# A transformer block with a state-space mixer, sparse attention and a mixture of experts: expert weights of four by row blocks and column quarters, the first w_in blocks in float32, powers by doubling

## The chip, the cores and the metric

The kernel runs on one core of a Trainium2 chip. A core has five engines with queues of their own: TensorE (PE, matrix products into PSUM; its weight loads are listed apart as PEld), VectorE (DVE), ScalarE (ACT), GpSimd (POOL) and SyncE (SP), which here issues nearly all DMA transfers. Each engine takes its instructions in order, and a semaphore holds an instruction back until what it reads is there. The metric is the device time of one execution in microseconds (us); smaller is better. All data are float32 in HBM.

## The reference

One layer over 256 tokens of width 1024, in four steps, cut to what matters:

```
mod = silu(c) @ ada_w + ada_b                 # six vectors of 1024: sh1, sc1, g1, sh2, sc2, g2
h = rms_norm(x) * (1 + sc1) + sh1
proj = h @ w_in                               # q, six kv parts, gates, u (state space), merge gates
x = x + g1 * (g_attn * (attn @ w_o) + g_ssm * (ssm @ ssm_w_o)) @ w_out
h = rms_norm(x) * (1 + sc2) + sh2
x = x + g2 * moe(h)                           # 32 experts in 4 groups, the top group, 2 experts of it
return rms_norm(x)
```

`ssm` is a diagonal complex recurrence over the tokens (32 groups, 64 states each), written by the kernel as short convolutions and a scan over powers of the diagonal. `attn` is compressed, selected and windowed attention. Each expert computes `(silu(x @ w_gate) * (x @ w_up)) @ w_down` with an inner width of 256. All 32 experts together have 96 MB of weights (3 MB each), and all of them are read in every execution.

## The kernel before

The program is one function, `hybrid`, and a planner of the framework turns it into one list per engine: it runs the program on simulated times and puts ready instructions in the order in which they come up there. So the order on an engine isn't the order of the lines, and an edit in one place can move instructions in others. Buffers are tiles of pools; a tile that takes the memory of an older one waits until all readers of the older one are done. `room` (L69) hands out loads of 1 MB in turn from a list of such slots (`set_rings`), and `load` (L92) issues the transfer on SP's queue.

*The front.* The loop at L128 issues eight modulation blocks (`ada1_k`, 1 MB: two vectors for one 128-wide slice of the model) and eight row blocks of the first four column groups of w_in (`slab`, 128x1024 each, two to a slot): u0, u1 (input of the state-space part), kc and vc (compressed keys and values). They share the five slots of `ringA`. The loop at L375 takes the row blocks k = 0 to 7 in turn. `mod_sum` (L236) multiplies the modulation block with silu(c), eight products in four column groups of TensorE at once, and `mod_end` (L245) turns the sums upright and makes the scale Gm and the shift modT. Then the normed input, turned earlier into xnT, becomes hf = xnT * Gm + modT (L378). Products of the projections are done in three passes of a faster 4-byte type, float32r: `mm3` (L286) adds high x high, high x low and low x high, for which hf is split into hTh and hTl (L379, L380) and the row block into a pair of `whi` and `wlo` halves (L382 on ScalarE, L383 on VectorE). Per row block these are eight triples of 256 columns. Later projections split their weights in the same way in `split` (L272 to L284).

Beside it the constants of the state-space part are made: VectorE and POOL build the discretised matrices (L418 to L531), `cmul` (L472 to L478) makes complex powers in a chain, six instructions each: `pows` to the fourth power (three products), `pk4` to the eighth power of that (seven) and two squarings `sq`. Vc gets 20 copies of 64x256 (L574 to L580), four on ScalarE and sixteen on VectorE. The front ends with the products of L563, which need U (the projections of u0 and u1) and Wt.

*The middle.* Keys, compression (`blk`, L710 to L719: four windows of keys and values, with a column of zeros that POOL sets), the scan, attention by four chunks (L862 on), and output projections, up to `wout`. A matrix `perm` (L976) orders the tokens; it is read at L1057.

*The experts.* Nine blocks (BLOCKS): seven quads of experts with 32 places each and two pairs with 64, in the order quad, quad, pair, quad, pair, four quads. The ring has 21 slots of 1 MB. For each expert a quad loads gate and up weights in two halves of four row blocks each (`egu`, [128, 4, 512]), all first halves and then all second ones, and the down weights in one tile (`edn`, [128, 2, 1024]): twelve loads. For the last quad the second halves come as two pieces of 512 KB per expert, and the down weights as two column halves. `ffn_block` (L1183) does, for each row block k, one product per expert (four side by side in TensorE's columns, L1192), the activation (L1200 to L1202), the down product in two halves of 512 columns (L1215), the weighting (L1218), and adds the result to the four accumulators `acc` (L1224). After the last block come the squares (L1317), the last norm and four output transfers (L1359).

```
for e, h in order_[:n_e] if last else order_:
    egu[e][h] = load(A["egu"][e0 + e][:, 4 * h:4 * h + 4], [4, 512], f"gu{e0 + e}{h}")
```

## Time and profile before

| | |
|---|---|
| median of three runs | 599.57 us (598.16 to 601.19) |
| the profiled execution | 600.95 us, span 599.1 us |
| TensorE busy | 526.7 us (88%) |
| VectorE busy | 343.1 us (57%) |
| ScalarE, POOL busy | 200.2 and 201.4 us (33 and 34%) |
| moved by DMA | 168.11 MB, mean 281 GB/s |
| mean granted TensorE clock | 0.963 |

The span runs from the first to the last instruction; the execution's own time is 1.85 us longer. A busy share is a mean over stages with different limits, so each stage is read by itself. In rows of instruction groups the columns are line, engine, operation, written tile and read tiles, shapes and count, then busy time and mean duration in ns, then the idle time just before them and what ended it. A float32 matmul is two records in the trace, one of float32r is one.

### The profile page before, as it was taken

The numbers are of one execution on the slowest core, as the hardware profiler recorded it, in microseconds if no ns is written. First come the engines' busy times: TensorE is split into PE (matmuls) and PEld (weight loads), VectorE is DVE, ScalarE is ACT, GpSimd is POOL, SyncE is SP. The second block draws the span as 40 slices with busy tenths as digits, with TensorE's granted clock in tenths as the row PEclk, the third lists the DMA queues.
The fourth block names the chain that finished last, engine by engine and source line by source line (L and its number), as shares of the span: only waits on it lengthen the run. The fifth ranks groups of instructions, "written<-read, shape, count | busy, mean of one in ns | idle before, by whom it ended". The sixth has DMA issues, their size and how long they took to land.

```text
span 599.1 us, 10825 instructions
## 1 busy us (share of the span) xinstructions
PE 526.7 (88%) x4173; PEld 369.1 (62%) x4174; DVE 343.1 (57%) x942; ACT 200.2 (33%) x461; POOL 201.4 (34%) x299
## 2 busy tenths in 40 slices
...
GB/s 328 318 259 143 220 132 123 354 209 275 157 198 185 133 107 75 266 171 127 112 363 392 244 323 370 264 339 422 418 418 421 421 421 420 420 419 421 413 344 74
DMA packets 28443, 168.11 MB, mean 281 GB/s; under 512 B 3171, under 2 KB 3299, under 8 KB 11363
## 3 DMA queue, kind: packets, MB, share of 16 engines
...
q14 instruction: 22, 0.17, 0.1%
...
## 4 chain that ended last, share of the span: by engine, by line
PE 52%; DVE 19%; issue 10%; DMA 8%; POOL 7%; ACT 3%; SPq 0%; POOLq 0%; ACTq 0%; DVEq 0%
PE guq L1192 9%; PE pgq L1163 5%; PE dnq L1215 5%; DMA adt<-in_adat_dram 4%; PE acc L1224 4%; DMA fg<-in_fg_dram 3%; POOL adt L354 2%; DVE wlo L282 2%; DVE wlo L383 2%; PE p L291 2%; PE p L290 2%; PE y L799 2%; PE p L289 2%; POOL pr L919 2%; DMA slab<-in_w_dram 1%
## 5 line engine op out<-in xcount | busy, mean ns | idle before, releaser
L1356 POOL TENSOR_TENSOR x<-x,fg 128x512 f32<-128x512 f32 x1 | 1.3, 1267 | 263.6 <-ACT x L1355 263.6
L1192 PE MATMUL guq<-gu,room__4521 128*32 128x512 f32 (+1 forms) x480 | 69.5, 611 | 3.2 <-DMA gu<-in_egu_dram 2.2
L1167 DVE TENSOR_SCALAR room__4521<-pgq,Gm,modT 128x128 f32<-128x128 f32 x36 | 14.7, 409 | 71.5 <-PE pgq L1163 36.2
L1163 PEld LDWEIGHTS pgq<-room__4521,x 128*128 128x128 f32 x288 | 37.9, 197 | 23.2 <-issue 10.1
L1165 ACT ACTIVATE room__4521<-pgq,modT,Gm 128x128 f32<-128x128 f32 x36 | 16.5, 460 | 98.7 <-PE pgq L1163 90.8
L1163 PE MATMUL pgq<-room__4521,x 128*128 128x128 f32 x288 | 45.0, 296 | 4.0 <-DVE room__4521 L1167 1.9
L1192 PEld LDWEIGHTS guq<-gu,room__4521 128*32 128x32 f32 (+1 forms) x480 | 18.0, 115 | 43.1 <-issue 34.8
L919 POOL TENSOR_SCALAR pr<-pr,st 128x128 f32<-128x128 f32 (+1 forms) x64 | 36.1, 579 | 24.8 <-DVE st L916 17.6
L354 POOL TENSOR_SCALAR adt<-adt,ct 128x256 f32<-128x256 f32 x64 | 36.2, 581 | 22.6 <-DMA adt<-in_adat_dram 22.5
L241 PE MATMUL pm<-ada,csb 128*32 128x256 f32 x256 | 22.2, 442 | 20.9 <-DVE csb L217 16.3
L1224 PE MATMUL acc<-gb,room__4521 128*128 128x512 f32 x72 | 33.5, 605 | 0.9 <-DVE gb L1218 0.9
L1215 PE MATMUL dnq<-ed,acq 128*32 128x512 f32 (+1 forms) x224 | 34.2, 597 | 0.0
L914 ACT ACTIVATE pr<-s,st 128x128 f32<-128x128 f32 (+1 forms) x64 | 26.2, 423 | 22.6 <-DVE st L910 21.8
L1201 DVE SCALAR_TENSOR_TENSOR pk<-pk,guq 128x256 f32<-128x256 f32 x9 | 3.8, 422 | 51.9 <-ACT pk L1200 51.9
L1218 DVE SCALAR_TENSOR_TENSOR gb<-dnq,wsq,gb 128x512 f32<-128x512 f32 x18 | 13.5, 751 | 31.9 <-PE dnq L1215 31.9
L1200 ACT ACTIVATE pk<-guq 128x256 f32<-128x256 f32 x9 | 3.5, 385 | 72.7 <-PE guq L1192 72.7
L1224 PEld LDWEIGHTS acc<-gb,room__4521 128*128 128x128 f32 x72 | 12.9, 189 | 20.9 <-issue 19.1
L241 PEld LDWEIGHTS pm<-ada,csb 128*32 128x32 f32 x256 | 7.9, 121 | 28.3 <-DVE csb L217 16.0
L355 POOL TENSOR_TENSOR adt<-adt 128x512 f32<-128x512 f32 x16 | 21.8, 1368 | 0.3
L291 PE MATMUL pj_gs<-hTh,wlo 128*128 128x256 f32 x64 | 19.2, 301 | 2.0 <-DVE wlo L282 2.0
L291 PE MATMUL p<-oTh,wlo 128*128 128x256 f32 x64 | 19.0, 296 | 1.5 <-DVE wlo L282 1.5
L289 PE MATMUL p<-oTh,whi 128*128 128x256 f32 x64 | 18.9, 295 | 0.8 <-ACT whi L281 0.8
...
## 6 DMA issues: line engine op xcount, KB each, us to landing
...
```

The lines of the kernel that those rows point to most:

```text
L241: T.matmul(pm_k[32 * t:32 * t + 32, 0:256], lhsT=csb[:, 2 * t + j], rhs=slot[:, 2 * t + j], start=j == 0, stop=j == 1, tile_position=(0, 3 ...
L289: T.matmul(o, lhsT=ah, rhs=bh, start=start, stop=False)
L291: pe_last[0] = T.matmul(o, lhsT=al, rhs=bh, start=False, stop=stop)
L354: G.tensor_scalar(w[:, t], w[:, t], ct[:, 4 * h + t:4 * h + t + 1], 1.0, op0=ALU.mult, op1=ALU.mult)
L355: G.tensor_add(w[:, 0:2], w[:, 0:2], w[:, 2:4])
L914: S.activation(pr[:, a_:b_], src, AF.Exp, bias=st[:, 1, z:z + 1], scale=0.125, accum_out=st[:, 2, z:z + 1])
L919: G.tensor_scalar(pr[:, a_:b_], pr[:, a_:b_], st[:, 3, z:z + 1], 1.0, op0=ALU.mult, op1=ALU.mult)
L1163: T.matmul(pg[:, k % 2, 0:S_], lhsT=x[:, b, 128 * k:128 * k + 128], rhs=O[:, b, 0:S_], start=b == 0, stop=b == 1)
L1165: S.activation(xe[:, k, 0:S_], pg[:, k % 2, 0:S_], AF.Identity, bias=sh2[:, k:k + 1], scale=G2[:, k:k + 1])
L1192: gl_ = T.matmul(gu[r], lhsT=xe[:, k, r], rhs=wgu(e, k), start=k == 0, stop=k == 7, tile_position=(0, s_ * e))
L1215: T.matmul(dn[r], lhsT=ac[:, c, r], rhs=wdn(e, c)[:, 512 * h:512 * h + 512], start=c == 0, stop=c == 1, tile_position=(0, s_ * e))
L1224: T.matmul(acc[b][h], lhsT=OT[0:M, sl], rhs=ty2[0:M, h], start=False, stop=last)
```

## The change

It has these parts:

- The first seven slots of the front's loads are the memory of `whi` and `wlo` and then the five of `ringA`.
- The first four column groups of w_in are multiplied in float32: hf with the row block as it is, eight products per row block in place of eight triples. The halves of the row block are no longer made; hTh and hTl are still made, for the later projections, hTh as a copy of hf. The modulation sums run two row blocks ahead, and the scaled input one.
- Powers are made by doubling (`times`): four instructions multiply one power with one, two or four others, seven calls in all.
- All copies into Vc are on ScalarE.
- The two `blk` tiles are made once, and VectorE sets their zeros.
- `perm` takes the memory of `onesc`, after its last reader.
- A quad's gate and up weights lie in HBM as eight row blocks with all four experts in each (`egq`), its down weights as four column quarters with all experts (`edq`), 1 MB each, and are loaded in that order, the last quad's too. The down product runs by quarters of 256 columns. In the last block the weighting and the sums run by quarters as well.

The diff, cut to its core:

```diff
@@ -125,6 +125,7 @@
...
     ada1, slab = [], []
+    set_rings([Late("whi"), Late("wlo")] + [ringA] * NA)
     for k in range(8):
@@ -372,23 +373,33 @@
...
     o4 += [bank(f"pj_{nm}", tag).rearrange("p (m t) -> p m t", m=2) for nm, tag in (("kc", "o"), ("vc", "s"))]
+    hfs = []
+
+    def rows(p_):
+
+        mod_end(*p_)
+        k = p_[3]
+        hf = pp.tile([128, 256], F32, name=f"hf{k}", tag="hf", bufs=3)
+        hfs.append(hf)
+        V.tensor_scalar(hf, xnT[:, k], Gm[:, 0, k:k + 1], modT[:, 0, k:k + 1], op0=ALU.mult, op1=ALU.add)
+        S.copy(hTh[:, k], hf)
+        V.tensor_sub(hTl[:, k], hf, f32(hTh[:, k]))
+
+
+    pms = [mod_sum(ada1[0], 0, 0, "s"), mod_sum(ada1[1], 0, 1, "s")]
+    rows(pms[0])
     for k in range(8):
-        mod_end(*mod_sum(ada1[k], 0, k, "s"))
-        hf = pp.tile([128, 256], F32, name=f"hf{k}", tag="hf", bufs=2)
-        V.tensor_scalar(hf, xnT[:, k], Gm[:, 0, k:k + 1], modT[:, 0, k:k + 1], op0=ALU.mult, op1=ALU.add)
-        S.activation(hTh[:, k], xnT[:, k], AF.Identity, bias=modT[:, 0, k:k + 1], scale=Gm[:, 0, k:k + 1])
-        V.tensor_sub(hTl[:, k], hf, f32(hTh[:, k]))
-        hi, lo = halves()
-        S.copy(hi, slab[k])
-        V.tensor_sub(lo, slab[k], f32(hi))
+        if k < 6:
+            pms.append(mod_sum(ada1[k + 2], 0, k + 2, "s"))
+        if k < 7:
+            rows(pms[k + 1])
+        hf, w4 = hfs[k], slab[k]
         for i in range(2):
             for b in range(2):
-                sl, c = slice(128 * b, 128 * b + 128), slice(256 * i, 256 * i + 256)
-                mm3(o4[i][:, b], hTh[:, k, sl], hTl[:, k, sl], hi[:, c], lo[:, c], k + b == 0, k + b == 8)
+                T.matmul(o4[i][:, b], lhsT=hf[:, 128 * b:128 * b + 128], rhs=w4[:, 256 * i:256 * i + 256], start=k + b == 0, stop=k + b == 8)
         for i in range(2, 4):
             for m in range(2):
-                c = slice(256 * i + 128 * m, 256 * i + 128 * m + 128)
-                mm3(o4[i][:, m], hi[:, c], lo[:, c], hTh[:, k], hTl[:, k], k + m == 0, k + m == 8)
+                pe_last[0] = T.matmul(o4[i][:, m], lhsT=w4[:, 256 * i + 128 * m:256 * i + 128 * m + 128], rhs=hf, start=k + m == 0, stop=k + m == 8)
     for i in range(2):
@@ -529,15 +540,26 @@
...
         S.copy(Wt[:, 2 * gq:2 * gq + 2].rearrange("p a b c -> p (a b) c"), pst)
-    for j in (2, 3, 4):
-        cmul(V, pows[:, j, 0], pows[:, j, 1], pows[:, j - 1, 0], pows[:, j - 1, 1], pows[:, 1, 0], pows[:, 1, 1], u1, u2)
+    pwt = pp.tile([128, 2, 4, 2, 16], F32, name="pwt")
+
+    def times(o, a, b):
+
+        n = b.shape[1]
+        p1, p2 = pwt[:, 0, 0:n], pwt[:, 1, 0:n]
+        for p_, r in ((p1, 0), (p2, 1)):
+            V.tensor_tensor(p_, a[:, r].unsqueeze(1).unsqueeze(2).to_broadcast([128, n, 2, 16]), b, op=ALU.mult)
+        V.tensor_sub(o[:, :, 0], p1[:, :, 0], p2[:, :, 1])
+        V.tensor_add(o[:, :, 1], p1[:, :, 1], p2[:, :, 0])
+
+    times(pows[:, 2:3], pows[:, 1], pows[:, 1:2])
+    times(pows[:, 3:5], pows[:, 2], pows[:, 1:3])
 
...
     V.tensor_copy(pk4[:, 1], pows[:, 4])
-    for k in range(2, 9):
-        cmul(V, pk4[:, k, 0], pk4[:, k, 1], pk4[:, k - 1, 0], pk4[:, k - 1, 1], pk4[:, 1, 0], pk4[:, 1, 1], u1, u2)
+    for n in (1, 2, 4):
+        times(pk4[:, n + 1:2 * n + 1], pk4[:, n], pk4[:, 1:n + 1])
     for r in range(2):
@@ -546,7 +568,7 @@
...
             sq, sq_ = pp.tile([128, 2, 16], F32, name=f"sq{i_}"), sq
-            cmul(V, sq[:, 0], sq[:, 1], sq_[:, 0], sq_[:, 1], sq_[:, 0], sq_[:, 1], u1, u2)
+            times(sq.unsqueeze(1), sq_, sq_.unsqueeze(1))
         V.tensor_copy(aS[:, i_, 0], sq[:, 0:1].to_broadcast([128, 2, 16]))
@@ -574,10 +596,7 @@
...
                 dst = Vc[ps_, :, r, 32 * j + 16 * hv:32 * j + 16 * hv + 16]
-                if j == 0:
-                    S.activation(dst, ccur[r][ps_], AF.Copy, scale=-1.0 if r else 1.0)
-                else:
-                    V.tensor_scalar(dst, ccur[r][ps_], -1.0 if r else 1.0, None, op0=ALU.mult)
+                S.activation(dst, ccur[r][ps_], AF.Copy, scale=-1.0 if r else 1.0)
 
@@ -653,6 +672,9 @@
...
     KV2 = cz.tile([128, 2, 4, 128], F32, name="KV2")
+    blks = [cz.tile([128, 2, 4, 4, 16], F32, name=f"blk{n}") for n in range(2)]
+    for blk in blks:
+        V.memset(blk[:, :, :, :, 15:16].rearrange("p k c g o -> p (k c g o)"), 0.0)
     for i, nm in enumerate(("kc", "vc")):
@@ -707,8 +729,7 @@
...
         tick(f"cw{n}")
-        blk = cz.tile([128, 2, 4, 4, 16], F32, name=f"blk{n}", tag="blk", bufs=2)
-        G.memset(blk[:, :, :, :, 15:16].rearrange("p k c g o -> p k c (g o)"), 0.0)
+        blk = blks[n % 2]
         for kd in range(2):
@@ -972,8 +993,6 @@
...
     mg = mgs.enter_context(tc.tile_pool(name="mg", bufs=1))
-    perm = mg.tile([128, 128], F32, name="perm")
-    V.tensor_scalar(perm, itok1[:, 0:128], tq, 1.0, op0=ALU.subtract, op1=ALU.is_equal)
     G2, sh2 = Gm[:, 1], modT[:, 2]
@@ -1004,6 +1023,8 @@
...
     S.copy(rbias, prb[:, 0:36])
+    perm = onesc
+    V.tensor_scalar(perm, itok1[:, 0:128], tq, 1.0, op0=ALU.subtract, op1=ALU.is_equal)
 
@@ -1207,21 +1228,27 @@
...
         S.activation(ac[:, :, 0:M], pa_[:, :, 0:M], AF.Copy, scale=0.5)
+        nz = 2 if n_e == 4 else 1
         for h in range(2):
             dn = (pmr if h else pm_).tile([128, 512], F32, name=f"dn{nm}{h}", tag=f"dn{h}")
-            for c in range(2):
-                for e in range(n_e):
-                    r = slice(s_ * e, s_ * e + s_)
-                    T.matmul(dn[r], lhsT=ac[:, c, r], rhs=wdn(e, c)[:, 512 * h:512 * h + 512], start=c == 0, stop=c == 1, tile_position=(0, s_ * e))
             ty = ty2[:, h]
-            for c in (slice(0, 512),):
-                act_last[0] = V.scalar_tensor_tensor(ty[0:M, c], dn[0:M, c], ws[0:M, 0:1], g2b[0:M, 512 * h + c.start:512 * h + c.stop], op0=ALU.mult, op1=ALU.mult)
+            for z in range(nz):
+                zs = slice(512 // nz * z, 512 // nz * (z + 1))
+                for c in range(2):
+                    for e in range(n_e):
+                        r = slice(s_ * e, s_ * e + s_)
+                        T.matmul(dn[r, zs], lhsT=ac[:, c, r], rhs=wdn(e, c, nz * h + z), start=c == 0, stop=c == 1, tile_position=(0, s_ * e))
+                if last or z == nz - 1:
+                    zs = zs if last else slice(0, 512)
+                    act_last[0] = V.scalar_tensor_tensor(ty[0:M, zs], dn[0:M, zs], ws[0:M, 0:1], g2b[0:M, 512 * h + zs.start:512 * h + zs.stop], op0=ALU.mult, op1=ALU.mult)
 
...
             for h in range(2):
-                for b in range(2):
-                    sl = slice(128 * b, 128 * b + 128)
-                    T.matmul(acc[b][h], lhsT=OT[0:M, sl], rhs=ty2[0:M, h], start=False, stop=last)
+                for z in range(2 if last else 1):
+                    zs = slice(256 * z, 256 * z + 256) if last else slice(0, 512)
+                    for b in range(2):
+                        sl = slice(128 * b, 128 * b + 128)
+                        T.matmul(acc[b][h][:, zs], lhsT=OT[0:M, sl], rhs=ty2[0:M, h, zs], start=False, stop=last and z == 1)
         if last:
@@ -1279,30 +1306,20 @@
...
             fg = load(A["fg"].to_broadcast([128, 1024]), [1024], "fg")
-        egu = [[None, None] for _ in range(n_e)]
-        order_ = [(e, h) for e in range(n_e) for h in range(2)] if n_e == 2 else [(e, h) for h in range(2) for e in range(n_e)]
-        for e, h in order_[:n_e] if last else order_:
-            egu[e][h] = load(A["egu"][e0 + e][:, 4 * h:4 * h + 4], [4, 512], f"gu{e0 + e}{h}")
-        if last:
-            for e in range(n_e):
-                egu[e][1] = room("gul", e, [4, 512])
-            for q in range(0, 4, 2):
-                for e in range(n_e):
-                    nc.sync.dma_start(egu[e][1][:, q:q + 2], A["egu"][e0 + e][:, 4 + q:6 + q])
-        if not last:
+        if n_e == 2:
+            egu = [[load(A["egu"][e0 + e][:, 4 * h:4 * h + 4], [4, 512], f"gu{e0 + e}{h}") for h in range(2)] for e in range(n_e)]
             edn = [load(A["edn"][e0 + e], [2, 1024], f"ed{e0 + e}") for e in range(n_e)]
         else:
-            edn = [room("edl", e, [2, 1024]) for e in range(n_e)]
-            for h in range(2):
-                for e in range(n_e):
-                    nc.sync.dma_start(edn[e][:, :, 512 * h:512 * h + 512], A["edn"][e0 + e][:, :, 512 * h:512 * h + 512])
+            egu = [load(A["egq"][(e0 - NW) // 4, k], [4, 512], f"gq{e0}{k}") for k in range(8)]
+            edn = [load(A["edq"][(e0 - NW) // 4, q], [8, 256], f"eq{e0}{q}") for q in range(4)]
         if i == 0:
...
                 O_ = masks(i + 1)
-        ffn_block(n_e, s_, wss[i], lambda e, k: egu[e][k // 4][:, k % 4], lambda e, c: edn[e][:, c], f"q{e0}", last,
-                  None if last else lambda: wss.append(prepared(i + 1)))
+        wgu = (lambda e, k: egu[e][k // 4][:, k % 4]) if n_e == 2 else lambda e, k: egu[k][:, e]
+        wdn = (lambda e, c, q: edn[e][:, c, 512 * q:512 * q + 512]) if n_e == 2 else lambda e, c, q: edn[q][:, 2 * e + c]
+        ffn_block(n_e, s_, wss[i], wgu, wdn, f"q{e0}", last, None if last else lambda: wss.append(prepared(i + 1)))
     _, cnt, cmx = rest_[0]
@@ -1344,7 +1361,7 @@
...
                             T.matmul(acc[b][h], lhsT=ident, rhs=ty2[:, b], start=True, stop=False)
-                    ffn_block(1, 64, slots(64, O, gm_, own[:, 0], nm), lambda e_, k: gu_[k // 4][:, k % 4], lambda e_, c: dn_[:, c], nm, True)
+                    ffn_block(1, 64, slots(64, O, gm_, own[:, 0], nm), lambda e_, k: gu_[k // 4][:, k % 4], lambda e_, c, q: dn_[:, c, 512 * q:512 * q + 512], nm, True)
         squares()
@@ -1407,6 +1424,9 @@
...
     o["edn"] = i["moe_w_down"][0].reshape(32, 2, 128, 1024).transpose(0, 2, 1, 3)
+    n = (NE - NW) // 4
+    o["egq"] = gu[NW:].reshape(n, 4, 8, 128, 512).transpose(0, 2, 3, 1, 4)
+    o["edq"] = i["moe_w_down"][0][NW:].reshape(n, 4, 2, 128, 4, 256).transpose(0, 4, 3, 1, 2, 5).reshape(n, 4, 128, 8, 256)
     o["rb"] = np.concatenate([i["moe_b_group"][0], i["moe_b_expert"][0]])[None]
```

## The prediction

> **What bounds the kernel now.** I read the page first, then the span cut into stages, then the groups of VectorE in the first stage, the chain of waits, and last the DMA queue's own waits. The page's slices show where the bytes move.
>
> ```profile
> PE 526.7 (88%) x4173; PEld 369.1 (62%) x4174; DVE 343.1 (57%) x942; ACT 200.2 (33%) x461; POOL 201.4 (34%) x299
> GB/s 328 318 259 143 220 132 123 354 209 275 157 198 185 133 107 75 266 171 127 112 363 392 244 323 370 264 339 422 418 418 421 421 421 420 420 419 421 413 344 74
> ```
>
> The last third runs at a flat 420 GB/s and nothing before it does. The same trace by stages (length, then busy time and instructions of PE, weight loads, DVE, ACT, POOL, then granted clock, DMA share, GB/s):
>
> ```profile
> 10.50:81.20 70.70, 53.10 (x403) 40.15 (x403) 68.02 (x286) 32.14 (x62) 30.51 (x40) 0.93 0.61 239
> 81.20:303.00 221.80, 203.77 (x2016) 177.33 (x2016) 164.39 (x372) 104.40 (x264) 141.47 (x209) 0.96 0.50 177
> 303.00:387.25 84.25, 78.70 (x611) 71.22 (x608) 56.63 (x143) 34.91 (x70) 24.20 (x34) 0.96 0.87 337
> 387.50:392.50 5.00, 5.00 (x48) 1.72 (x44) 0.69 (x5) 0.00 (x0) 0.00 (x0) 1.00 0.21 46
> 392.50:582.50 190.00, 179.15 (x1084) 76.60 (x1076) 40.46 (x113) 21.64 (x50) 0.00 (x0) 0.99 1.01 416
> 583.00:599.10 16.10, 6.32 (x22) 1.74 (x20) 5.00 (x23) 3.45 (x9) 1.27 (x1) 0.80 0.19 71
> ```
>
> Five stages, five limits. Up to 81.2 us (first projection, constants of the state-space part) **VectorE** is busy 68.0 of 70.7 us. From 81.2 to 387 TensorE is busy 92 to 93%, in a chain that passes through all engines, with DMA at half load at first. From 387.5 to 392.5 the DMA stands nearly still: every slot of the expert ring is full. From 392.5 to 582.5 the **DMA** share is 1.01: this stage is bytes over rate, whatever TensorE does. After the last byte (about 582.8, from the windows further down) comes a serial tail of 16.3 us.
>
> So a microsecond won before 387 moves everything behind it; one won between 392.5 and 582.5 counts only if it moves the start, the bytes' rate or the tail.
>
> **The change, part by part.**
>
> *Front: what VectorE loses.*
>
> ```profile
> L383 DVE TENSOR_TENSOR wlo<-slab,whi 128x1024 fp32r<-128x1024 f32 x8 | 10.3, 1288 | 0.2 <-ACT whi L382 0.2
> L580 DVE TENSOR_SCALAR Vc<-b 64x256 f32<-64x256 f32 x16 | 6.3, 391 | 0.1
> L473 DVE TENSOR_TENSOR u<-pk 128x16 f32<-128x16 f32 x8 | 2.7, 332 | 0.1
> L475 DVE TENSOR_TENSOR pk<-u,u 128x16 f32<-128x16 f32 x7 | 2.5, 357 | 0.2
> L478 DVE TENSOR_TENSOR pk<-u,u 128x16 f32<-128x16 f32 x7 | 2.2, 316 | 0.2
> L476 DVE TENSOR_TENSOR u<-pk 128x16 f32<-128x16 f32 x8 | 2.2, 274 | 0.2
> L474 DVE TENSOR_TENSOR u<-pk 128x16 f32<-128x16 f32 x8 | 1.8, 221 | 0.0
> L477 DVE TENSOR_TENSOR u<-pk 128x16 f32<-128x16 f32 x8 | 1.3, 167 | 0.0
> ```
>
> The eight low halves of w_in (L383) go: 10.3 us. The sixteen copies into Vc go to ScalarE: 6.3 us. The six rows of the powers hold 46 instructions in 12.7 us, 0.28 each; all 72 (12 products of 6) are about 20. The new form is 7 products of 4, 28 instructions on up to 128 columns; no such product is in the trace, so between 28 x 0.17 = 4.7 (the shortest row) and 28 x 0.36 = 10 us (the longest); I take 8, since wider ones fall among the slow. That removes 12. Together 28.6 of 68.0: VectorE is left with about 39.4 us, and could be done at 50. It stops being the bound. ScalarE loses eight casts of 128x1024 and gets sixteen copies of 64x256 instead, of a size with those that VectorE lost; at 32.1 of 70.7 us busy it hides them.
>
> *Front: what TensorE gains.* Per row block of w_in, 24 passes in float32r become 8 products in float32, each of two records. The prices, from the timeline (eleven float32r matmuls in a row, and a modulation product after a pause) and from the chain of waits:
>
> ```profile
> 79.03 0.28 PE L290 MATMUL pj_kc<-hTl,whi 128*128 128x256 f32 x1
> ...
> 80.23 0.28 PE L291 MATMUL pj_vc<-hTh,wlo 128*128 128x256 f32 x1
> ```
>
> ```profile
> 37.55 1.94 PE L241 MATMUL pm<-ada,csb 128*32 128x256 f32 x16 [3.47 <-DVE mr L251]
> ```
>
> ```profile
> 144.41 1.00 PE pm L241 x16
> 413.62 3.63 PE acc L1224 x8
> ```
>
> ```profile
> L530 PE MATMUL pst<-ident,bw 128*128 128x128 f32 x32 | 4.5, 278 | 0.5 <-ACT Wt L531 0.5
> L249 PE MATMUL pm<-ident,msk 128*128 128x128 f32 x16 | 3.6, 322 | 0.6 <-ACT msk L243 0.6
> ```
>
> Ten steps in 1.20 us: 0.12 per pass, 0.36 for a triple. Eight float32 records of 512 columns take 3.63, so 0.454 for two records of 256. One float32 product costs 26% more than the triple that it replaces: 64 x 0.094 = 6.0 us more for TensorE. The Trainium skill, FP8 and Floating Point Precision, TensorE Precision Notes, speaks harder against this edit: float32 is four passes, so 4/3 of three passes, or 0.48; by it the stage would end 1.7 us later; the trace's 0.454 decides.
>
> TensorE then needs per row block 8 x 0.454 = 3.63, 1.00 for the modulation and 3.6/8 = 0.45 for its transposes: 5.08. Eight are 40.6, less two modulations that run ahead (2.0), plus 4.5 for the transposes of L530: 43.1 us. It can begin when the first hf is there. In the chain:
>
> ```profile
> 12.16 1.23 DVE wlo L383
> ...
> 18.06 1.14 DVE wlo L383
> ...
> 24.26 0.32 DVE hf L378
> ```
>
> Two low halves (2.4 us) lie ahead of that hf and vanish: 22.2. With 43.1 us at the 0.93 of this stage (46.3) the outputs of L563 can start near 68.5 instead of 81.2. The modulations run two row blocks ahead, and the split of hTh (now a copy of hf) is off this path. The loads should not be later: with two ring slots more, five modulation blocks and four slabs land unasked; the last modulation block takes the slot of slabs 2 and 3, free after the fourth row block (22.2 + 4 x 5.08/0.93 = 44 us), and is wanted one block later, near 49. I take **-12.7**, bounds -6 (a row block stalls 0.8 us on a load or on VectorE's order) and -17 (full clock, no gap).
>
> *Middle.* Memsets of blk go from POOL to VectorE (0.15 us each, under 81.2 to 303 where both wait often), perm is computed later in onesc (a 128x128 operation under wout; VectorE is idle 27 of 84 us there). Nothing in this stretch waits for anything but work, so the shift passes. Its order is planned anew, though: 0, bounds -4 to +5.
>
> *Experts: the first free slot.* The DMA queue's waits from 378 to 396, its timeline and the chain there:
>
> ```profile
> SPq L95 <- PE guq L1192: 9.1, 2, 6.8
> SPq L95 <- PE acc L1057: 5.2, 1, 5.2
> SPq L1324 <- DVE m L1240: 3.8, 1, 3.8
> ```
>
> ```profile
> 390.90 1.29 SPq L95 DMA_DIRECT2D ed<-in_edn_dram  x3
> ```
>
> ```profile
> 387.25 3.64 PE guq L1192 x32
> ```
>
> Today all four tiles of the first half are read until the fourth row block, so four slots free at 390.9. By row blocks the first frees after a quarter of 3.64, at 388.2, and one more every 0.91 us, while a megabyte takes 2.5 us at 416 GB/s: **-2.7**, bounds 0 and -4. The wait for acc L1057 (which reads perm) goes, but is worth nothing: all 21 slots are full by 387.5 with it. Within the quads the down product is 32 matmuls of 256 instead of 16 of 512: sixteen records of 256 cost 1.00 (above), so 4.0 instead of 3.6 us, hidden by the DMA stage.
>
> *Experts: the end.* Windows, then the timeline:
>
> ```profile
> 571.00:581.00 10.00, 7.15 (x33) 1.38 (x32) 1.48 (x3) 0.77 (x2) 0.00 (x0) 1.00 1.04 387
> 581.00:583.00 2.00, 0.47 (x2) 0.14 (x2) 0.11 (x1) 0.00 (x0) 0.00 (x0) 1.00 0.71 257
> 583.00:585.00 2.00, 2.00 (x6) 0.68 (x4) 0.00 (x0) 0.27 (x1) 0.00 (x0) 1.00 0.06 20
> ```
>
> ```profile
> 575.71 0.42 DVE L1202 TENSOR_TENSOR pk<-pk,guq 128x256 f32<-128x256 f32 x1
> ...
> 583.51 1.99 PE L1224 MATMUL acc<-gb,room__4521 128*128 128x512 f32 x4
> ...
> 585.42 1.91 PE L1215 MATMUL dnq<-edl,acq 128*32 128x512 f32 x12
> ...
> 588.21 1.98 PE L1224 MATMUL acc<-gb,room__4521 128*128 128x512 f32 x4 [0.88 <-DVE gb L1218]
> ...
> 590.29 0.60 ACT L1317 ACTIVATE room__4521<-acc 128x512 f32<-128x512 f32 x1 [0.17 <-PE acc L1224]
> 590.79 0.20 ACT L1317 ACTIVATION_READ_ACCUMULATOR room__4521<-acc 128x1 f32 x1
> ```
>
> The last 8.4 MB today come in half pieces at 387 GB/s (21.7 us); as whole 8 KB rows at 420, 20.0: **-1.5**, bounds 0 and -1.7. After the last byte at 582.8 the order is sums of the first half, down products of the second, weighting, its sums and squares until 591.0: 8.2 us. With column quarters the last piece leaves one product of sixteen records (1.0), a weighting of 256 (0.42), four records of sums (1.0) and the squares of two halves (0.8 each with the read-out), with about 0.5 between: 4.5, so **-3.7**; bounds -2 (an earlier quarter's sums stand ahead, and more gaps) and -4.5.
>
> *Sum.* The profiled execution took 600.95 (span 599.1 and 1.85 around it), 1.4 over the median. 600.95 - 12.7 - 2.7 - 1.5 - 3.7 = 580.35; on the median's footing 579.0. I say **579**.
>
> **The rivals.**
>
> *The front's gain is eaten in the middle.* The order between 81 and 303 is planned from simulated times, and another front gives another order. For: that stretch is a chain over all engines, where one queue's order can cost microseconds. Against: its DMA share is 0.50 and no row shows a wait on a clock or on bytes only. Then the expert part alone counts: 599.6 - 7.9 = 591.7.
>
> *Only the front counts.* The slots free in a row but the DMA restarts no earlier, since the queue stands at the register load L1324 (a wait of 3.8 us there), and the last pieces end as before. Against: that wait ends with L1240, before 384. 599.6 - 12.7 = 586.9.
>
> *The front is faster than TensorE's sum.* TensorE at full clock, VectorE at 50, the middle better by 4 too: 599.6 - 17 - 4 - 7.9 = 570.7. The Trainium skill, TensorE: Matmul & The Clock Gate, Part 1, bears on this: half speed until some 3.4 us of steady work; a front with fewer pauses would then hold full clock; by it the front ends at 22.2 + 43.1 = 65.3 and the time is 576; the trace agrees, in that the product at 37.55 costs 1.94 after a pause of 3.47 us and 1.00 elsewhere.
>
> *Slower: TensorE becomes the bound at half rate.* The row at 37.55 shows the price doubled. If loads or VectorE's order leave pauses between all row blocks, 43.1 us become 86.2 and L563 starts at 108.4, 27.2 later: 599.6 + 27.2 - 7.9 = 618.9. It turns into a loss once the mean granted clock over the front is under 43.1/(81.2 + 7.9 - 22.2) = 0.64. Against: 0.93 now, with more pauses.
>
> **How the numbers follow.** Forecast 0.55; gain eaten 0.20; only the front 0.10; faster front 0.09; slower 0.06. All but the last lie below the present time, though 0.03 of the eaten case (the middle 5 us worse, half the expert part) comes within 0.5% (3 us), which is about what can be told from no change here. Faster 0.91, same 0.03, slower 0.06. All good ends at once give 599.6 - 17 - 4 - 4 - 1.7 - 4.5 = 568.4, all bad ones 599.6 - 6 + 5 - 2 = 596.6. The range is 567 to 593: the good ends with a microsecond, the eaten case with one, and it leaves out the slow case and the worst of the bad ends.
>
> **What would show it.** VectorE under 45 us busy before L563; L563 starting between 64 and 75; 128 float32 records of the first projection about 0.21 us apart; the first load after the full ring within 1.2 us of the first expert product; DMA at 415 GB/s and more to its end; under 13 us from the last byte to the end. The forecast is wrong if L563 starts after 76, if 81 to 387 is not 306 us long within 5, or if the DMA's full stage is not about 188 us.

## The result and the profile after

The changed kernel took 582.55 us (median of four runs, 581.25 to 584.24) beside 598.87 us for the kernel before in the same series (597.05 to 601.19): a ratio of 0.973, 95% interval 0.968 to 0.977. The forecast was 579 (567 to 593). The time came out well; two of the steps behind it, the middle and the tail, did not. Of the runs further down, two of one kernel (the float32r triples, 592.41 and 593.03 us) count as slow and are left out of its median and its ratio.

The profiled execution took 581.25 us, its span 579.5. From its page, the busy times and the bytes in 40 slices:

```profile
PE 514.7 (89%) x4341; PEld 370.0 (64%) x4342; DVE 320.4 (55%) x878; ACT 196.7 (34%) x469; POOL 200.1 (35%) x295
GB/s 322 415 344 156 192 91 290 212 217 309 193 143 182 103 81 180 221 146 155 211 379 350 218 417 355 286 422 422 419 419 421 420 421 420 419 420 420 422 316 76
```

The same stages as before, each from its own first instruction (columns as in the prediction's table of stages; the fourth is the pause of the DMA, the fifth its full stage, the sixth the tail):

```profile
10.50:69.45 58.95, 49.70 (x338) 37.46 (x339) 45.00 (x219) 29.54 (x70) 28.33 (x40) 0.94 0.73 287
69.45:291.30 221.85, 206.49 (x2055) 180.66 (x2054) 169.81 (x384) 107.24 (x275) 145.82 (x211) 0.97 0.52 185
291.30:369.85 78.55, 72.54 (x571) 65.39 (x569) 51.09 (x130) 31.49 (x59) 20.75 (x27) 0.98 0.88 340
367.50:372.50 5.00, 4.39 (x42) 2.22 (x44) 2.35 (x13) 0.91 (x2) 0.00 (x0) 1.00 0.21 48
372.50:562.00 189.50, 175.14 (x1306) 81.32 (x1302) 40.75 (x117) 21.56 (x50) 0.00 (x0) 0.96 1.01 418
562.00:579.50 17.50, 8.14 (x60) 4.33 (x52) 5.73 (x25) 3.22 (x9) 1.27 (x1) 0.79 0.19 68
```

Finer windows show the DMA's rate fall near 562.5 (205, 57 and 25 GB/s in the three microseconds from 561), as it fell near 582.8 before. The table takes these two times for the last weights, as the prediction did. So, span against span:

| stretch | before | after | moved | forecast |
|---|---|---|---|---|
| up to the first x product (L563, now L585) | 81.2 | 69.45 | -11.7 | -12.7 |
| from there to the first expert product | 306.05 | 300.4 | -5.65 | 0 |
| first expert product to the last weights | 195.55 | 192.65 | -2.9 | -4.2 |
| last weights to the end | 16.3 | 17.0 | +0.7 | -3.7 |
| sum | 599.1 | 579.5 | -19.6 | -20.6 |

The sum agrees because 5.65 us that nobody forecast stand in for most of the 6.7 us that did not come (1.0 in the front, 1.3 and 4.4 in the experts).

The profile also gives the time of each load from its issue to its landing, and by it both ends are later. The last weights of the kernel before were issued at 572.87, those of the changed kernel at 544.29:

```profile
edl<-in_edn_dram SPq DMA_DIRECT2D x1, 512.0 KB, 12.3
```

```profile
eq<-in_edq_dram SPq DMA_DIRECT2D x1, 1024.0 KB, 19.8
```

So they were there at 585.2 and 564.1. Counted from these times the third row of the table is -3.7 and the fourth +1.5. Three questions follow: what made the front shorter, where the middle's gain came from, and what held the tail.

The first one starts from a row of TensorE's timeline in the front, which shows a new pause, with the products after it at half pace (8 records in 3.78 us; the next row block's 8 take 1.73 in the chain of waits):

```profile
40.44 3.78 PE L399 MATMUL pj_u<-slab,hf 128*128 128x256 f32 x8 [3.81 <-DVE hf L384]
```

The slots behave as forecast. The DMA queue's timeline shows the first load into a freed slot, 1.12 us after the first expert product (3.65 before):

```profile
369.85 2.35 PE L1213 MATMUL guq<-gq,room__4329 128*32 128x512 f32 x20 [0.55 <-ACT room__4329 L1186]
```

```profile
370.97 2.58 SPq L95 DMA_DIRECT2D eq<-in_edq_dram  x3
```

And the tail, from TensorE's timeline:

```profile
551.73 1.93 PE L1213 MATMUL guq<-gq,room__4329 128*32 128x512 f32 x8 [1.38 <-DMA gq<-in_egq_dram]
554.22 1.94 PE L1213 MATMUL guq<-gq,room__4329 128*32 128x512 f32 x8 [0.56 <-DMA gq<-in_egq_dram]
557.66 0.66 PE L1228 MATMUL paq<-ident,pk 128*128 128x128 f32 x2 [1.50 <-DVE pk L1223]
558.79 1.93 PE L1240 MATMUL dnq<-eq,acq 128*32 128x256 f32 x16 [0.47 <-ACT acq L1230]
561.33 1.93 PE L1240 MATMUL dnq<-eq,acq 128*32 128x256 f32 x16 [0.61 <-DVE gb L1243]
563.20 1.96 PE L1251 MATMUL acc<-gb,room__4329 128*128 128x256 f32 x4
565.08 1.07 PE L1240 MATMUL dnq<-eq,acq 128*32 128x256 f32 x16
566.09 1.13 PE L1251 MATMUL acc<-gb,room__4329 128*128 128x256 f32 x4
567.15 1.07 PE L1240 MATMUL dnq<-eq,acq 128*32 128x256 f32 x16
568.15 1.99 PE L1251 MATMUL acc<-gb,room__4329 128*128 128x256 f32 x8
```

The last down product (567.15) starts 3.0 us after its weights landed. What sets the end is a chain on TensorE that begins with the last row block at 554.22. Up to 565 it runs at half pace (16 records in 1.93 us against 1.07 later), and the second quarter waits 0.61 us for the weighting (L1243) of the first, which reads the same PSUM tile.

### The profile page after: what moved, and what is told of

The parts are those of the page before. It is cut to its first block, busy times and chain, and to the rows that moved or that the text cites. A ratio compares the mean times of both kernels' runs of the same rounds, so it can differ in the third digit from the quotient of the medians.

```text
span 579.5 us, 11082 instructions
## 1 busy us (share of the span) xinstructions
PE 514.7 (89%) x4341; PEld 370.0 (64%) x4342; DVE 320.4 (55%) x878; ACT 196.7 (34%) x469; POOL 200.1 (35%) x295
## 3 DMA queue, kind: packets, MB, share of 16 engines
q1 hardware_dynamic: 23906, 158.97, 69.5%
## 4 chain that ended last, share of the span: by engine, by line
PE 63%; DVE 17%; issue 9%; DMA 5%; POOL 3%; ACT 2%; POOLq 0%; ACTq 0%
PE guq L1213 9%; PE pgq L1184 5%; PE dnq L1240 5%; PE acc L1251 4%; DMA fg<-in_fg_dram 3%; DVE wlo L283 2%; PE po L957 2%; PE p L292 2%; PE p L291 2%; PE p L290 2%; PE y L820 2%; PE pj_u L399 2%; PE pta L945 1%; PE x L290 1%; PE x L291 1%
## 5 line engine op out<-in xcount | busy, mean ns | idle before, releaser
L1213 PE MATMUL guq<-gq,room__4329 128*32 128x512 f32 x448 | 56.2, 626 | 7.7 <-DMA gq<-in_egq_dram 6.8
L355 POOL TENSOR_SCALAR adt<-adt,ct 128x256 f32<-128x256 f32 x64 | 38.7, 622 | 21.6 <-DMA adt<-in_adat_dram 20.5
L1213 PEld LDWEIGHTS guq<-gq,room__4329 128*32 128x32 f32 x448 | 12.3, 111 | 37.5 <-issue 17.5
L1243 DVE SCALAR_TENSOR_TENSOR gb<-dnq,wsq,gb 128x512 f32<-128x512 f32 (+1 forms) x20 | 13.9, 697 | 38.5 <-PE dnq L1240 38.5
L1251 PE MATMUL acc<-gb,room__4329 128*128 128x512 f32 (+1 forms) x80 | 34.9, 576 | 0.0
L1240 PE MATMUL dnq<-eq,acq 128*32 128x256 f32 x448 | 33.7, 401 | 1.1 <-DVE gb L1243 0.6
L242 PE MATMUL pm<-ada,csb 128*32 128x256 f32 x256 | 18.2, 415 | 14.8 <-DVE csb L218 14.8
L1251 PEld LDWEIGHTS acc<-gb,room__4329 128*128 128x128 f32 x80 | 14.7, 196 | 19.2 <-issue 18.9
L1240 PEld LDWEIGHTS dnq<-eq,acq 128*32 128x32 f32 x448 | 14.2, 113 | 12.5 <-issue 1.8
L399 PE MATMUL pj_u<-slab,hf 128*128 128x256 f32 x64 | 17.6, 418 | 5.0 <-DVE hf L384 4.0
```

Source lines behind the costliest of these rows:

```text
L242: T.matmul(pm_k[32 * t:32 * t + 32, 0:256], lhsT=csb[:, 2 * t + j], rhs=slot[:, 2 * t + j], start=j == 0, stop=j == 1, tile_position=(0, 3 ...
L355: G.tensor_scalar(w[:, t], w[:, t], ct[:, 4 * h + t:4 * h + t + 1], 1.0, op0=ALU.mult, op1=ALU.mult)
L399: T.matmul(o4[i][:, b], lhsT=hf[:, 128 * b:128 * b + 128], rhs=w4[:, 256 * i:256 * i + 256], start=k + b == 0, stop=k + b == 8)
L1213: gl_ = T.matmul(gu[r], lhsT=xe[:, k, r], rhs=wgu(e, k), start=k == 0, stop=k == 7, tile_position=(0, s_ * e))
L1240: T.matmul(dn[r, zs], lhsT=ac[:, c, r], rhs=wdn(e, c, nz * h + z), start=c == 0, stop=c == 1, tile_position=(0, s_ * e))
L1251: T.matmul(acc[b][h][:, zs], lhsT=OT[0:M, sl], rhs=ty2[0:M, h, zs], start=False, stop=last and z == 1)
```

## The experiments

All start from the changed kernel, and the ratio is to the kernel before, measured beside it in five rounds. The columns between are from one profiled execution each (us): start of the first x product, from there to the first expert product, from that to the end of the last square.

| kernel | x starts | middle | experts | median | ratio, interval |
|---|---|---|---|---|---|
| before | 81.2 | 306.1 | 203.6 | 598.87 | 1 |
| changed | 69.5 | 300.4 | 201.1 | 582.55 | 0.973, 0.968 to 0.977 |
| five ring slots | 72.6 | 306.0 | 200.8 | 589.04 | 0.982, 0.978 to 0.986 |
| powers in a chain | 78.5 | 306.0 | 200.9 | 594.05 | 0.992, 0.989 to 0.995 |
| float32r triples | 69.8 | 308.3 | 200.9 | 586.8 | 0.979, 0.974 to 0.984 |
| blk and perm | 69.3 | 302.8 | 199.2 | 581.63 | 0.973, 0.971 to 0.976 |
| experts as before | 69.7 | 307.8 | 203.1 | 588.66 | 0.983, 0.979 to 0.986 |
| banks | 69.0 | 299.8 | 198.8 | 582.31 | 0.975, 0.972 to 0.978 |
| filler products | 69.3 | 303.0 | 199.8 | 582.77 | 0.976, 0.973 to 0.980 |
| late powers | 69.8 | 306.8 | 200.7 | 584.44 | 0.977, 0.974 to 0.980 |
| pr on ScalarE | 70.2 | 301.5 | 200.3 | 581.8 | 0.971, 0.967 to 0.975 |
| powers after hf | 70.0 | 304.0 | 198.8 | 584.35 | 0.976, 0.972 to 0.980 |
| banks and filler | 69.7 | 302.7 | 199.7 | 582.49 | 0.972, 0.968 to 0.975 |
| the last version | 69.2 | 299.9 | 201.6 | 580.43 | 0.967, 0.964 to 0.971 |

The middle alone moves by 8 us from kernel to kernel, and so do single runs of one kernel (the five-slot kernel: 582.6 to 590.6). So front and experts are read from the stages, and a median only with the middle in mind. How far one execution can be trusted is seen from kernels that share a part. In the nine with the changed front the first x product starts at 69.0 to 70.2. In the eight with the changed expert part (down to float32r triples, then blk and perm, late powers, pr on ScalarE, powers after hf) the column of the experts runs from 198.8 to 201.1.

### Five ring slots

```diff
-    set_rings([Late("whi"), Late("wlo")] + [ringA] * NA)
```

> The changed kernel with the front's loads in the five slots of ringA again, all else as changed. Theory (the front is VectorE's order and TensorE's sum, the two slots only keep loads out of the way): the modulation blocks 5 to 7 are issued later, TensorE stops once or twice for a load, L585 starts 1 to 4 us later than 69.5, the whole is 583 to 587 us. Rival (the two slots are what makes the front faster): L585 starts near 76 or later and the whole is 589 or more. Rival (slots are worth nothing): 582.5 within 1.

Without the two extra slots the x products start 3.2 us later, as the theory had it. The median is above its 583 to 587 because the middle was long (306.0). The slots do not save time by themselves: a slab is now held until its products are done, and the next run shows that with the triples five slots are enough.

### Float32r triples

```diff
-        hf, w4 = hfs[k], slab[k]
+        hi, lo = halves()
+        S.copy(hi, slab[k])
+        V.tensor_sub(lo, slab[k], f32(hi))
...
-                T.matmul(o4[i][:, b], lhsT=hf[...], rhs=w4[...], ...)
+                mm3(o4[i][:, b], hTh[...], hTl[...], hi[:, c], lo[:, c], ...)
```

The five slots are part of this kernel.

> The changed kernel with the triples in float32r, the halves of the row blocks and the five slots of before (the memory of whi and wlo is needed for the halves), but with the powers by doubling, the copies on ScalarE and the modulations two ahead. Theory (VectorE sets the front; the halves are 10.3 of its 28.6 us less): L585 at 73 to 79 us, the whole 586 to 592. Rival (TensorE sets the front, and the triples are 6 us shorter for it): L585 at 66 or earlier, and the whole 580 or less. Rival (the float32 products alone are the gain): L585 at 81, the whole 594.

The theory fell, and so did both rivals. Groups of VectorE in the first 70 us, and that stage in windows:

```profile
L397 DVE TENSOR_TENSOR wlo<-slab,whi 128x1024 fp32r<-128x1024 f32 x8 | 9.8, 1221 | 3.1 <-ACT whi L396 3.1
```

```profile
10.50:69.80 59.30, 46.26 (x376) 37.01 (x377) 51.52 (x226) 32.07 (x68) 28.98 (x35) 0.88 0.73 284
```

The halves are back with 9.8 us of VectorE, and the x products start at 69.8 all the same. Float32 with its two slots is worth nothing to the front here. TensorE is busy 46.3 us instead of 49.7, VectorE 51.5 instead of 45.0. So this run exchanges two things at once: what the halves cost by themselves, without the 3.4 us that TensorE saves, isn't shown. With five slots on both sides the triples are 2.8 us faster than float32 (69.8 against 72.6).

### Powers in a chain

```diff
-    for n in (1, 2, 4):
-        times(pk4[:, n + 1:2 * n + 1], pk4[:, n], pk4[:, 1:n + 1])
+    for k in range(2, 9):
+        cmul(V, pk4[:, k, 0], pk4[:, k, 1], pk4[:, k - 1, 0], pk4[:, k - 1, 1], pk4[:, 1, 0], pk4[:, 1, 1], u1, u2)
```

(and so for `pows` and `sq`)

> The changed kernel with the twelve complex powers as chains of six instructions again (72 in place of 28 on VectorE). Theory: VectorE has about 12 us more to do before the projection's end; it has 13 us of slack between 50 and 69 us, but its order puts powers ahead of hf, so the pause of TensorE before the third or fourth row block grows from 3.8 to 6 to 12 us: L585 at 72 to 78, the whole 585 to 591. Rival (the powers lie in VectorE's slack): L585 within 1 us of 69.5 and the whole 582.5 within 1.5.

The x products start at 78.5, a little beyond the theory's 78: the powers are worth 9 of the 11.7 us. VectorE's and TensorE's rows say how:

```profile
10.50:78.50 68.00, 51.42 (x338) 38.34 (x338) 56.83 (x263) 29.59 (x70) 27.09 (x40) 0.90 0.64 250
```

```profile
62.25 1.94 PE L242 MATMUL pm<-ada,csb 128*32 128x256 f32 x16 [8.61 <-DVE mr L252]
```

VectorE isn't full (56.8 of 68.0 us). Most of the loss is one pause: TensorE waits 8.6 us for mr, the first step of a row block's modulation, which starts at 62.04. From 47.12 to there VectorE's list holds nothing but the chain of powers and the tables made of it.

### blk and perm

```diff
+        blk = cz.tile([128, 2, 4, 4, 16], F32, name=f"blk{n}", tag="blk", bufs=2)
+        G.memset(blk[:, :, :, :, 15:16].rearrange("p k c g o -> p k c (g o)"), 0.0)
...
+    perm = mg.tile([128, 128], F32, name="perm")
```

> The changed kernel with the zeros of blk set by POOL inside the loop and perm in memory of its own before the output projections, as before. Theory (the 5.7 us won between L585 and the first expert product are a new order on POOL and ScalarE, not these edits): the stretch stays at 300 us within 2, the whole at 582.5 within 2.5. Rival (blk or perm was the cause): the stretch is 304 to 306 us and the whole 586 to 588.5. By both, the DMA refills the ring later (perm's reader holds a slot), which moves nothing.

The middle (302.8) lies between what the theory and the rival gave. The median, 581.63, speaks against the rival (586 to 588.5): these two edits don't seem to have brought the 5.65 us. One execution alone can't tell, as the spread of one program further down shows.

### Experts as before

Layout, loads and products of the experts are those of the kernel before.

> The changed kernel with the expert weights laid out, loaded and multiplied as before (per expert, halves of the gate and up weights, pieces for the last quad), front and middle as changed. Theory: from the first expert product to the last byte 195.5 us instead of 192.4, and from the last byte to the end 16.3 instead of 17.2, so together 2.2 us more: 583.5 to 586. Rival (the layout carries the gain): 588 or more. Rival (it is worth nothing): 582.5 within 1.

From the first expert product to the last square it takes 203.1 instead of 201.1 us. With the 198.8 to 201.1 of the eight kernels above, the expert part is worth 2 to 4 us, where the forecast had 7.9. The rest of this kernel's 6 us is its middle (307.8). Yet up to that point its instructions stand in the same order on TensorE, VectorE, ScalarE and GpSimd as in the changed kernel, so their order cannot be the cause.

### Late powers

```diff
+    with tc.issue_after(pe_k5.ins):
         times(pows[:, 2:3], pows[:, 1], pows[:, 1:2])
...
```

> The changed kernel with the powers and the tables made of them issued behind the sixth row block's products. Theory (VectorE's order puts powers and tables ahead of hf, which stops TensorE for 3.8 us before 40.4 and lets its clock drop for the 4 us behind): the pause goes, L585 starts 3 to 6 us earlier than 69.5, the whole is 577 to 580. Rival (other VectorE work, the state-space matrices, stands there instead): the pause stays within 1 us and the whole at 582.5 within 1.5. Rival (the late powers hold up the scan or the memory of the next loads): the front is earlier but the keys or the scan later, and the whole is 582 or more.

The planner made the same list for every engine as for the changed kernel, instruction by instruction, so this tells nothing of the pause. It is worth more as a second sample of the changed program: 584.44 us (582.96 to 587.28), and the profiled execution at 587.28 with a middle of 306.8 instead of 300.4. GpSimd's waits in the two, from 140 to 320 us, first the changed kernel, then this one:

```profile
POOL adt L355 <- DMA adt<-in_adat_dram: 17.4, 6, 6.1
```

```profile
POOL adt L355 <- DMA adt<-in_adat_dram: 21.9, 6, 6.2
```

And the timelines of GpSimd where they part, in the same order:

```profile
251.46 0.57 POOL L353 DMA_DIRECT2D adt<-in_adat_dram  x1 [0.30 <-DVE st L937]
...
256.35 2.96 POOL L355 TENSOR_SCALAR adt<-adt,ct 128x256 f32<-128x256 f32 x4 [0.59 <-DMA adt<-in_adat_dram]
```

```profile
254.93 0.57 POOL L353 DMA_DIRECT2D adt<-in_adat_dram  x1 [0.30 <-DVE st L941]
...
263.64 2.43 POOL L355 TENSOR_SCALAR adt<-adt,ct 128x256 f32<-128x256 f32 x3 [4.42 <-DMA adt<-in_adat_dram]
```

One 512 KB load takes 4.9 us from its issue to its reader in one execution and 8.7 in the other. In both it shares the engines with a 1 MB load of nwo that SP issues 0.9 us later (252.36 and 255.82). The Trainium skill, DMA: Bandwidth & Descriptors, Queues, rings and completion order, says that an engine goes round its queue rows packet by packet; that fits two queues in each other's way, but no run here shows the packets' turns. Behind that load on GpSimd stand the attention's probabilities (pr), and TensorE waits for these 1.8 us in one execution and 3.7 in the other (its waits from 140 to 380 us, each time two rows):

```profile
PE pta L945 <- POOL pr L940: 1.8, 2, 0.9
PE y L820 <- issue: 1.2, 2, 0.9
```

```profile
PE pta L949 <- POOL pr L944: 3.7, 2, 3.5
PE y L824 <- issue: 3.3, 2, 2.8
```

The second row of each is a pause with no releaser in the profile, 2.1 us longer here. The two differences are 4.0 of the 6.4 us. The rest is TensorE's pace. The middle of each in one window:

```profile
69.45:369.85 300.40, 279.03 (x2624) 246.05 (x2622) 220.90 (x514) 138.73 (x333) 166.57 (x238) 0.97 0.61 225
```

```profile
69.83:376.63 306.80, 281.72 (x2623) 249.22 (x2621) 218.00 (x514) 138.72 (x333) 165.26 (x238) 0.96 0.60 221
```

The same products keep TensorE busy 2.7 us longer at a granted clock of 0.96 instead of 0.97, and it is idle 3.7 us longer. The kernel before has 4.0 and 3.0 us in the same two waits and 282.5 us of busy TensorE in its middle, much like this second sample. So the middle's 5.65 us are within what two executions of one program differ by, and whether the change has a part in them stays open.

### pr on ScalarE

```diff
-                    G.tensor_scalar(pr[:, a_:b_], pr[:, a_:b_], st[:, 3, z:z + 1], 1.0, op0=ALU.mult, op1=ALU.mult)
+                    S.mul(pr[:, a_:b_], pr[:, a_:b_], st[:, 3, z:z + 1])
```

> From the changed kernel; the attention's probabilities (pr) are scaled by ScalarE instead of GpSimd: 64 small multiplications that stood on GpSimd between the sums of the adat pieces. Two profiled executions of one and the same program (the changed kernel, and the run with the late powers, whose instructions stood in the same order on every engine) had a stretch from the first x product to the first guq product of 300.3 and 306.8 us; GpSimd waited 17.4 and 21.9 us for its adt loads in them, and TensorE 1.8 and 3.7 us for pr. Theory: the middle's length is set by how late the adt loads land, because pr stands behind them on GpSimd. Then TensorE's waits for pr fall below 1 us, po lasts 107.5 us or less from first to last, the stretch is 300 us or less, the median 577 to 582, and single runs lie within 4 us of each other. Rival 1 (the granted clock and the issue pauses of TensorE decide): the waits for pr go, but the stretch stays at 300 to 307 and the median at 582 to 585. Rival 2 (ScalarE, which scales 64 times at about 0.42 us, the duration of its 64 exponentials, becomes the bound): po lasts over 112 us, TensorE or VectorE waits for ScalarE, and the median is over 585.

No wait of TensorE for pr is left, and GpSimd's waits for adt, now 35.6 us, hold nobody. The middle was 301.5 in this execution and 299.9 in that of the last version, which has the same edit; single runs lie in 580.1 to 584.0 and 579.3 to 581.9, where ten runs of the changed program lie in 581.25 to 587.28. Po lasts 108.6 us, so ScalarE doesn't bind. That speaks for the theory, though the stretch and po lie just above its bounds (300 and 107.5). But two executions are few, the medians' intervals overlap with the changed kernel's, and the kernel with banks, whose pr is on GpSimd and holds TensorE for 3.0 us, had a middle of 299.8.

### Powers after hf

```diff
-    V.tensor_copy(pk4[:, 1], pows[:, 4])
+    V.scalar_tensor_tensor(pk4[:, 1], hfs[3][:, 0:32]..., 0.0, pows[:, 4], op0=ALU.mult, op1=ALU.add)
```

> From the changed kernel; the powers from the fifth on take a zero times the fourth row block's hf into their first factor, so that they cannot start before that hf is made, and 4.5 us of VectorE's work (tables and doublings) stand behind it instead of ahead of it. (Issuing them later in the order had moved nothing.) Theory: TensorE's pause of 3.81 us ahead of the fourth row block, and the half clock after it (8 products in 3.78 us instead of 1.9), come from the powers ahead of that hf on VectorE. Then the pause falls to 2 us or less, the products of that block take about 1.9 us, and the first x product starts 2 to 4 us earlier, at 65.5 to 67.5 instead of 69.45. Rival 1 (GpSimd's tables, which need the powers, or the last row block's ada sum set the first x product): the pause falls, but the first x product stays at 69 to 71. Rival 2 (the pause comes from the chain of the modulation itself): the pause stays at 3 us or more. The median moves by the first x product's shift alone, under the middle's own spread of some 6 us.

From TensorE's timeline:

```profile
37.73 1.99 PE L399 MATMUL pj_u<-slab,hf 128*128 128x256 f32 x8 [0.88 <-DVE hf L384]
...
44.63 3.78 PE L399 MATMUL pj_u<-slab,hf 128*128 128x256 f32 x8 [3.17 <-DVE hf L384]
```

The pause goes where the powers go: the fourth row block now starts after 0.88 us at full pace, and the fifth waits 3.17 us, behind the doublings that were moved, at half pace. So the cause of the pause is shown, and the first x product gains nothing (70.0). It stays where rival 1 had it, but not for rival 1's reason: the pause has only moved. VectorE's list has a lump of work somewhere ahead of some hf.

### Banks

```diff
+                if last and z:
+                    dn = pmr.tile([128, 512], F32, name=f"dn{nm}{h}{z}", tag=("pg", "gu")[h])
```

> The changed kernel with a PSUM bank for each of the four column quarters of the last quad (the quarters of a half share one as changed, and the second waits until the first is weighted). Theory (the tail is a chain of four quarters on TensorE, at half its clock, with a wait for the weighting between quarters): the waits of 0.6 and about 0.4 us go and the next quarter overlaps the weighting: the last square ends 1 to 2.5 us earlier behind the last byte, the whole 580 to 581.5. Rival (order and clock alone make the tail, not the waits): the tail stays at 17.2 us within 0.4, 582.5 within 0.8.

From TensorE's timeline:

```profile
557.08 3.22 PE L1242 MATMUL dnq<-eq,acq 128*32 128x256 f32 x32 [0.47 <-ACT acq L1230]
560.23 1.48 PE L1253 MATMUL acc<-gb,room__4329 128*128 128x256 f32 x4
561.64 1.07 PE L1242 MATMUL dnq<-eq,acq 128*32 128x256 f32 x16
562.64 1.13 PE L1253 MATMUL acc<-gb,room__4329 128*128 128x256 f32 x4
563.70 1.07 PE L1242 MATMUL dnq<-eq,acq 128*32 128x256 f32 x16
564.70 1.99 PE L1253 MATMUL acc<-gb,room__4329 128*128 128x256 f32 x8
```

The second quarter follows the first without a wait, and the experts take 2.3 us less. But only 0.6 of that is the wait. Nearly all of the rest are rows that run at full pace here and at half pace in the changed kernel, and that differs between executions without any edit of the tail. The kernel of the section above, whose expert part is the changed kernel's, also takes 198.8, with the wait in it:

```profile
561.88 1.56 PE L1240 MATMUL dnq<-eq,acq 128*32 128x256 f32 x16 [0.47 <-ACT acq L1230]
564.03 1.89 PE L1240 MATMUL dnq<-eq,acq 128*32 128x256 f32 x16 [0.58 <-DVE gb L1243]
565.85 1.13 PE L1251 MATMUL acc<-gb,room__4329 128*128 128x256 f32 x4
```

So the wait is shown to go, and a gain of more than its 0.6 us is not. The median (582.31; the profiled execution, 578.04, is the fastest of six) doesn't move.

### Filler products

After each row block of the last quad one product of ident and x into a free bank, two after the eighth; its result isn't used.

> The changed kernel with extra products in the last quad (the identity with a part of x, into a free bank that nothing reads), one behind each row block and two behind the eighth, which does nothing but keep TensorE at work. Theory (pauses of 1 to 1.6 us at each row block of the last quad drop the granted clock to 0.7): the clock from 540 to 565 rises to 0.95 or more, the sixteen records of a quarter take 1.0 instead of 1.9 us, the last square ends 2 to 4 us earlier behind the last byte, the whole 578.5 to 580.5. Rival (the clock falls for another reason or the tail waits on data): clock or tail stay, 582.5 or, with the extra products in the way, up to 584.

Windows of the changed kernel and of this one:

```profile
540.00:560.00 20.00, 11.64 (x66) 1.96 (x66) 0.84 (x2) 0.77 (x2) 0.00 (x0) 0.70 1.01 420
```

```profile
540.00:560.00 20.00, 18.08 (x85) 4.30 (x84) 0.84 (x2) 0.67 (x2) 0.00 (x0) 1.00 1.01 419
```

The clock stays full, and the experts take 1.4 us less, under the 2 to 4 that were expected. That too is inside the 198.8 to 201.1 of the unedited tail, and the median (582.77) doesn't move. The plan changed with the edit: each quarter's sums now follow its products at once and wait 0.6 us for the weighting.

### Banks and filler, and the last version

> From the changed kernel; both edits of the tail together: the second quarters of the last four experts' down products get banks of their own, and filler products (ident by x, into a free bank) run after each row block of the last four experts, so that TensorE does not pause for the transfers. Alone they shortened the stretch from the first guq to the last square by 2.5 and 1.5 us. Theory: they do different things (one takes the waits for the weighting, 0.6 us each, out of the serial chain, the other the half clock), so together 3.5 to 5 us: the stretch is 196 to 197.6 us instead of 201.1, the granted clock from 540 to 560 is 1.0 instead of 0.70, the down products follow each other without a pause of 0.6 us, and the median is 577.5 to 579.5. Rival (the last transfer's bytes, which end near 562.5, and the fixed work behind them bind already): no more than with the banks alone, 198.5 us, and a median of 580 to 582.

The two together gave 199.7, about as the filler alone (199.8), short of the theory and of the rival. In this plan too each quarter's products are followed at once by its own sums, which wait 0.61 us for the weighting, four times over; a bank of its own removes nothing there. The last version has both edits, pr on ScalarE, and this:

```diff
         if last:
-            sums()
+            with tc.issue_after(dn_last[0].ins):
+                sums()
```

> From the changed kernel; three edits: ScalarE scales the attention's probabilities, filler products after each row block of the last four experts, and banks of their own for the second quarters together with all four quarters' down products ahead of all their sums on TensorE (in the kernel with both edits of the tail each quarter's products were followed at once by its own sums, which waited 0.61 us each for the weighting, so the banks did nothing). Theory (the tail is a serial chain of TensorE from the last row block on, with the weightings' waits in it and a granted clock of 0.70 ahead of it; the middle's spread comes from probabilities that stand behind adt on GpSimd): no wait for the weighting between the last quarters; the last square ends 12.5 to 13.5 us after the start of the last row block's guq products (16.8 in the changed kernel, 15.4 with both edits of the tail, whose four waits of 0.61 us are gone), so first guq to last square 197 to 198; the middle 300 to 302; the median 576 to 579, and single runs within 4 us. Rival 1 (the end is bound by the last transfer and by work after it that isn't TensorE's, so the banks and the order give nothing): 199.6 us to the last square and a median of 580 to 582. Rival 2 (the middle's spread isn't GpSimd's; the median of the run with ScalarE alone was low by chance): the middle 303 to 307 and a median of 579 to 584.

From TensorE's timeline:

```profile
557.21 1.07 PE L1249 MATMUL dnq<-eq,acq 128*32 128x256 f32 x16 [0.47 <-ACT acq L1236]
558.64 1.07 PE L1249 MATMUL dnq<-eq,acq 128*32 128x256 f32 x16 [0.36 <-SPq L1352]
561.13 1.07 PE L1249 MATMUL dnq<-eq,acq 128*32 128x256 f32 x16 [1.42 <-SPq L1352]
563.52 1.78 PE L1249 MATMUL dnq<-eq,acq 128*32 128x256 f32 x16 [1.32 <-SPq L1352]
565.23 4.65 PE L1260 MATMUL acc<-gb,room__4329 128*128 128x256 f32 x16
```

My theory of the tail fell in its second half, and rival 1 gave the reason though not the number (201.6). The last three products start 2.4 to 2.5 us apart, the time of a megabyte at 420 GB/s. The waits are put down to SP's register load, which had long been done. By their time from issue to landing the weights of these three were there at 558.5, 561.0 and 563.5, and each product starts within 0.15 us of that: it is the weights they wait for. TensorE stood idle between them while the sums it could have done were ordered behind. The banks' order was better: there the last product starts at 563.70, 0.7 us after its weights landed, and 3.8 us later the squares are done (here 7.2). Still this version's median, 580.43, is the lowest of all. Its interval ends at 0.971 and so lies below the second sample of the changed kernel (from 0.974), though not below the first (from 0.968). Its gain comes with the middle, and the banks' tail with its middle would be the next version; that was not run.

## Why the prediction was right or wrong

*Front, -12.7; measured -11.7.* Right in size, and its account only in part. The path that I added up is there: the first product of the projections starts at 23.24 (forecast 22.2) and the first x product 46.2 us later (forecast 46.3). Inside it two errors cancel. I counted no pause, and there is one of 3.8 us; and TensorE's work without pauses and half pace is some 39.5 us, where I had 43.1. A part of that is the price: I took 0.454 for a float32 product of 256 columns, and the chain has 4 records in 0.86, 0.43 per product. The Trainium skill's four passes (FP8 and Floating Point Precision, TensorE Precision Notes), which gave 0.48 beside it, are further off. The rate halved by pauses, of which I warned, came behind that one pause and cost nearly 3 us, about what the clock of 0.93 in my sum stands for.

I also listed the halves' 10.3 us and the powers' 12 us alike as relief of VectorE. With the chain the powers cost 9 us; with the triples the halves are back and the front is as fast. In the changed front VectorE's sum is not the bound: what counts is what stands in its list ahead of the next hf. For the kernel before, where VectorE was busy 68.0 of 70.7 us, no run shows which of the two it was. Neither the copies into Vc nor the lead of the modulations was undone, so the 2.7 us that the powers leave are not divided.

*Middle, 0 with -4 to +5; measured -5.65.* By the prediction's own sign (306 us within 5) the forecast is wrong here: the stretch was 300.4 in this execution. The bounds allowed for a new order, and left out that one program shows 300.4 and 306.8. What the change itself does to the middle stays open. I also wrote that no row showed a wait on bytes only. There was one: the chain of waits of the kernel before has these two steps, GpSimd's adt again.

```profile
240.80 7.10 DMA adt<-in_adat_dram
...
263.32 9.06 DMA adt<-in_adat_dram
```

*First slot, -2.7; measured -2.5.* Right, by its own mechanism.

*Rate of the last megabytes, -1.5; measured about -0.4 by the fall of the rate* (2.9 from the first expert product to the last weights, less 2.5), *and -1.2 by the landings* (3.7 less 2.5). The term was a little too large. I put 387 GB/s on all of the last 8.4 MB, but the ten microseconds before the window that I quoted ran at 409, so only about 1 us was to be had.

*Tail, -3.7; measured +0.7.* This step failed, in two places. The first is a reading: at 582.8 the last weights were not there yet. They landed at 585.2, so 2.4 of the 8.2 us up to the last square at 591.0 were still the transfer, and against the forecast's 4.5 only 1.3 us were to be had. The second is the order: I said that after the last byte one product, a weighting and the sums remain. In the changed kernel these were not the last to be ready: the last quad's row blocks arrive 2.5 us apart and take 1 us at full pace, the clock falls to 0.70 in between, and TensorE's serial chain from the last row block reaches the last quarter 3.0 us after its weights landed. The sum itself was not too small: from the start of that product to the last square it takes 3.8 us, in the changed kernel and with the banks alike. How late the product starts varies from 0.8 to 3.1 us in the eight kernels with this expert part, with the half pace in the chain.

The rivals: the front's gain was not eaten, and the faster front and the half rate over the whole front did not come. Nearest in number is "only the front counts" (586.9): without the middle's 5.65 the profiled execution would be 586.9 (581.25 + 5.65), and the second sample's was 587.28. That is a coincidence, since this rival had the slots free no earlier, and they did (2.5). The 579 was 3.5 us off in the median. The steps without the middle were 6.7 us off and the middle made up for most of it. As far as the runs tell, that was luck: the second sample of the same program gained 13.2 us in the median (584.44 beside 597.63), near the 13.95 of front, experts and tail.
